# Moving GpSimd's arithmetic of a four-layer diffusion trunk to VectorE and ScalarE, RWKV's r, k and v as four-pass products, and its decay without own token as a shifted copy

## The chip, the core and the metric

The kernel runs on one core of one Trainium2 chip. The metric is the device time of one execution in microseconds; the time before is the median of three runs. Engines are named as the profile names them: PE is TensorE's matmul, PEld its weight load, DVE VectorE, ACT ScalarE, POOL GpSimd and SP the SyncE queue, which issues most DMAs.

## What is computed

One serving step of a trunk of four layers over 128 context and 128 latent tokens (two "sequences" s) of width 1024, all in float32. Layer 0 mixes tokens by a gated DeltaNet, layer 1 by neighbourhood attention, layer 2 by latent attention, layer 3 by RWKV-7; each layer ends in a SwiGLU feed-forward network. What bears on the change:

```
deltanet: q, k, v, z = split(h @ w_in); q, k, v = silu(dwconv3(q, k, v)); q, k = l2norm(q) * d**-0.5, l2norm(k)
          o = chunked gated delta rule, both directions (a triangular solve in it)
          out = (rmsnorm(o, out_norm) * silu(z)) @ w_out
rwkv:     xx = mean of both neighbours - h;  x_i = h + xx * mu_i   for i = r, k, v, w, a, g
          r, k, v = x_r @ W_r, x_k @ W_k, x_v @ W_v;  w, a, g by low-rank products (loras)
          decay = exp(-KAPPA * sigmoid(w)), cumulated over the tokens; vector-valued delta state, both directions
attention: p = softmax(s);  o = p @ v
```

## The kernel before

The program first records all its instructions on a tape, and a planner (class `Plan`) then sets the order of issue on each engine: a list schedule by rank (length of the rest of the chain) over costs that `Plan.costs` gives to each instruction, with pools of tiles (`ROOM`: 25 of 1024 columns, 28 of 512, seven PSUM banks) as a limit. So every instruction's engine and cost bear on the order of all of them. Each engine works through its instructions in order. All instructions are issued from one line (L2040), so the rows are told apart by shape, not by line.

**Products.** A large product runs as three passes of a faster matmul type (`F32R`): both sides are split into a rounded part `hi` (ScalarE copy) and a rest `lo` (VectorE, `raw - hi`), and hi·hi, hi·lo and lo·hi are summed in PSUM. `split` (L261) and `weight` (L270) do so for weights, `split_T` (L361) for activations. `linear` (L292) walks over chunks of 512 outputs and k; `linear_k` (L319) over k outermost with four accumulators (two sequences by two halves of 512). `linear_k` does RWKV's r, k and v projections (`project`, 8 k-tiles of 128x1024 each) and the second half of each feed-forward network. Products of plain float32 operands, as the loras', run as four passes, which the trace shows as two records.

```
nc.tensor.matmul(acc[s][c], xh, hi[:, 0, w], start=(k == 0), stop=False)
nc.tensor.matmul(acc[s][c], xh, lo[:, 0, w], start=False, stop=False)
...
nc.tensor.matmul(acc[s][c], xl, hi[:, 0, w], start=False, stop=(k == nk - 1))
```

**DeltaNet** (`deltanet_`, L626). After a chunk of q, k or v is projected, `evac` (L722) transposes it, copies it to SBUF (ScalarE), forms the convolution's middle and left tap on VectorE and the right one in two steps on GpSimd, takes SiLU, transposes back, and copies the result on VectorE. z is multiplied by the output norm's gain on GpSimd. `decays` (L761) adds a mask to four tiles of 128x1024, `unit` (L774) scales q, both on GpSimd. `inverses` (L572) inverts triangular blocks: a forward substitution of 31 steps, two VectorE instructions each (`substitute`, L524), between stream transposes, then small-tile products (`inverse_64`, L541) whose result VectorE negates.

**Attention** (`attend`, L915). Twelve calls in each of the two attention layers; each ends by copying the transposed probabilities from PSUM on VectorE.

**RWKV** (`rwkv_`). From the normed rows it forms `hx` and `xx`, and at once the split mix for k (`mk`). `mixed` forms x_i for one half g of the columns: on VectorE four instructions of 128x256, on GpSimd two of 128x1024; GpSimd has the loras' second half and all of r and v (`POOLMIX`). `mixes` splits them. Then: loras w and a; k projection; `rw_decays` (cumulative sum, and exponentials with and without the own token); `rw_keys`; r projection; lora g; `rw_products`; the inverse of the first half of the heads; v projection; queries; `rw_core` twice, with `fill` (the modulation's weights) between; the second half of the heads; the output products. `rw_keys` (half of it), `rw_queries` and the bonus in `rw_out` run on GpSimd.

Of the kernel before, what the change touches and what calls it, by code (L numbers as in the profile page):

```python
# [96 lines left out]
class Trunk:  # L97
# [163 lines left out]
    def split(self, raw, shape, pool=False):  # L261
# [4 lines left out]
        (nc.gpsimd if pool else nc.vector).tensor_tensor(lo, raw, hi.bitcast(F32), op=OP.subtract)  # L266
        self.free(raw)
        return hi, lo

    def weight(self, pieces, nk, width, pool=False):  # L270
# [7 lines left out]
        return self.split(raw, [128, nk, width], pool)  # L278
# [13 lines left out]
    def linear(self, W, chunks, xs, evac, lags=None, pool=()):  # L292
# [7 lines left out]
        for s, t in steps:  # L300
            ci, k0, n = units[t]
            width = sum(b - a for a, b in chunks[ci])
            if t not in held:
                held[t] = self.weight([W[k0 * 128:(k0 + n) * 128, a:b] for a, b in chunks[ci]], n, width, t in pool)
# [14 lines left out]
    def linear_k(self, W, xs, evac, lags=None, done=None, pool=()):  # L319
# [6 lines left out]
        for s, k in self.order(nk, 2, lags):  # L326
            if k not in held:
                held[k] = self.weight([W[k * 128:(k + 1) * 128, :]], 1, 1024, pool=k in pool)
            hi, lo = held[k]
            xh, xl = xs[s](k)  # L330
            for c in range(2):
                w = slice(c * 512, c * 512 + 512)
                nc.tensor.matmul(acc[s][c], xh, hi[:, 0, w], start=(k == 0), stop=False)
                nc.tensor.matmul(acc[s][c], xh, lo[:, 0, w], start=False, stop=False)
            for c in range(2):
                w = slice(c * 512, c * 512 + 512)
                nc.tensor.matmul(acc[s][c], xl, hi[:, 0, w], start=False, stop=(k == nk - 1))
# [15 lines left out]
    def to_T(self, src, n, hi, lo):  # L353
# [5 lines left out]
        self.split_T(p, n, hi, lo)  # L359

    def split_T(self, p, n, hi, lo):  # L361

        v = p[:, :n * 128].rearrange("p (a b) -> p a b", b=128)
        self.nc.scalar.activation(hi, v, AF.Copy)
        self.nc.vector.tensor_tensor(lo, v, hi.bitcast(F32), op=OP.subtract)
# [139 lines left out]
class DeltaNet:  # L505
# [35 lines left out]
    def inverse_64(self, Dc, DTc, AT, up, out):  # L541
# [13 lines left out]
        with self.scope():  # L555
# [10 lines left out]
            for B in range(2):  # L566
                a, b = (2 * B, 2 * B + 1) if not up else (2 * B + 1, 2 * B)
                c = 32 * (b % 2)
                nc.vector.tensor_scalar(out[32 * a:32 * a + 32, :, c:c + 32],
                                        py[32 * a:32 * a + 32, :].rearrange("p (m c) -> p m c", c=32), -1.0, None, op0=OP.mult)  # L570
# [55 lines left out]
    def deltanet_(self, l):  # L626
# [5 lines left out]
        r = self.g([72, 128])  # L632
        nc.gpsimd.dma_start(r, I["dn_conv"][j].rearrange("w (c p) -> (w c) p", p=128))
        p = self.ps()
        nc.tensor.transpose(p[:, :72], r, self.ident[:72, :72])
        cw = self.g([128, 3, 24])
        nc.vector.tensor_copy(cw.rearrange("p w c -> p (w c)"), p[:, :72])
# [6 lines left out]
        ona = self.g([128, 128])  # L644
        self.bcast_row(ona, I["dn_out_norm"][j])
# [7 lines left out]
        nc.gpsimd.tensor_tensor(wgl, wg, wgh.bitcast(F32), op=OP.subtract)  # L653
# [68 lines left out]
        def evac(ci, s, ps):  # L722
            which, half = ci // 2, ci % 2
            if which == 3:
                nc.scalar.activation(zs[s][half].rearrange("p a b -> p (a b)"), ps, AF.Silu)
                nc.gpsimd.tensor_tensor(zs[s][half], zs[s][half], ona[:, None, :].to_broadcast([128, 4, 128]), op=OP.mult)
                return
            with self.scope():
# [5 lines left out]
                x = self.g([128, 4, 128])  # L734
# [6 lines left out]
                y = self.g([128, 4, 127])  # L741
                nc.gpsimd.tensor_tensor(y, x[:, :, 1:], cw[:, 2, ci * 4:ci * 4 + 4, None].to_broadcast([128, 4, 127]), op=OP.mult)
# [1326 lines left out]
```

## Time and profile before

| | |
|---|---|
| median of 3 runs | 1763.6 us (1759.65 to 1768.04) |
| profiled execution | 1756.56 us, span 1754.6 us |
| mean granted TensorE clock | 0.952 |
| busy: PE, DVE, ACT, POOL | 1606.4, 1222.1, 826.5, 209.9 us |
| arithmetic on POOL | 89 TENSOR_TENSOR, 146.9 us |

The profile is of one execution. Busy is the time in which an engine had an instruction under way; a window is a stretch of the span, with the busy time of each engine in it. The clock is the share of 2.4 GHz that was granted to TensorE. A group of instructions has its busy time, the mean of one, and the idle time just before them with what ended it.

### The profile page before, as it was taken

The page shows a single profiled execution, that of the slowest core. Times are in us where ns is not written, and L with a number is a line of the kernel's source. Part 1 is how long each engine was busy: PE and PEld are TensorE (multiplying, and loading weights), DVE is VectorE, ACT ScalarE, POOL GpSimd, SP SyncE. Part 2 cuts the span into 40 slices and gives each one's busy share as a digit, 9 for nine tenths or more (in the row PEclk, how much of TensorE's full clock was granted, in tenths as well). Part 3 has the DMA queues.
Part 4 walks back from the last instruction along what each step waited for, and adds up shares of the span by engine and source line. Part 5 has one row for each costly group of instructions (what it writes and reads, how often), then busy time and mean ns, then how long its engine had stood idle before and what let it go on. Part 6 is the DMA issues. An engine that isn't in the chain of part 4 may idle for free. (4 is left out here: it accounts for less than half of the span.)

```text
span 1754.6 us, 25240 instructions
## 1 busy us (share of the span) xinstructions
PE 1606.4 (92%) x9492; PEld 1240.1 (71%) x9492; DVE 1222.1 (70%) x2369; ACT 826.5 (47%) x1400; POOL 209.9 (12%) x198
## 2 busy tenths in 40 slices
PE   6988799999999999999999999997729969989998
PEld 2765377887777778877777788875527858868886
DVE  3798888554596885446899744578986897585454
ACT  3666255443464564334665543444423722454343
POOL 2235110000002000000000000013630521000000
PEclk9989889999999999999999999998869879999999
DMA  9524959536567885366686744571511241336453
GB/s 360 186 90 139 363 189 325 195 129 210 208 256 242 304 295 181 131 216 232 243 340 211 253 156 161 203 264 49 193 59 50 83 150 49 121 103 204 156 181 132
DMA packets 130602, 333.86 MB, mean 190 GB/s; under 512 B 18305, under 2 KB 32450, under 8 KB 119216
## 3 DMA queue, kind: packets, MB, share of 16 engines
q1 hardware_dynamic: 123888, 311.33, 50.4%
q0 software_dynamic: 6592, 20.92, 3.9%
q8 instruction: 74, 1.21, 0.3%
q14 instruction: 48, 0.39, 0.1%
HBM read 328.31 MB, written 3.90 MB: 189 GB/s over the span
## 5 line engine op out<-in xcount | busy, mean ns | idle before, releaser
L2040 PE MATMUL v<-v,v 128*128 128x512 f32 (+11 forms) x9460 | 1598.7, 368 | 139.0 <-DVE v L2040 90.1
L2040 PEld LDWEIGHTS v<-v,v 128*128 128x128 f32 (+5 forms) x9460 | 1234.1, 172 | 502.2 <-DVE v L2040 120.7
L2040 DVE TENSOR_TENSOR v<-v,v 128x1024 fp32r<-128x1024 f32 (+19 forms) x1258 | 909.2, 748 | 452.2 <-ACT v L2040 267.5
L2040 ACT ACTIVATE v<-v 128x1024 fp32r<-128x1024 f32 (+13 forms) x991 | 694.2, 737 | 867.3 <-PE v L2040 392.9
L2040 POOL TENSOR_TENSOR v<-v,v 128x512 f32<-128x512 f32 (+3 forms) x89 | 146.9, 1671 | 227.3 <-ACT v L2040 127.4
L2040 POOL DMA_DIRECT2D v<-v x22 | 12.0, 548 | 666.9 <-PE v L2040 373.9
L2040 ACT ACTIVATE v<-v,v,v 128x128 f32<-128x128 f32 (+2 forms) x136 | 55.4, 474 | 28.1 <-DVE v L2040 27.3
L2040 ACT ACTIVATE v<-v,v 128x128 f32<-128x128 f32 (+1 forms) x144 | 52.7, 426 | 28.7 <-DVE v L2040 20.5
L2040 DVE TENSOR_SCALAR v<-v,v 128x128 f32<-128x128 f32 (+2 forms) x116 | 48.5, 456 | 10.1 <-ACT v L2040 9.6
L2040 DVE SCALAR_TENSOR_TENSOR v<-v,v,v 128x128 f32<-128x128 f32 (+3 forms) x120 | 51.4, 479 | 1.2 <-PE v L2040 0.9
L2040 DVE TENSOR_SCALAR v<-v 128x4 int32<-128x4 int32 (+10 forms) x206 | 43.7, 218 | 12.2 <-ACT v L2040 8.2
L2040 DVE TENSOR_REDUCE v<-v 128x4 f32<-128x512 f32 (+4 forms) x76 | 46.6, 626 | 5.1 <-ACT v L2040 2.6
L2040 POOL MEMSET v<- 128x512 f32 (+3 forms) x26 | 15.5, 614 | 250.4 <-PE v L2040 125.0
L2040 DVE COPY v<-v 128x512 f32<-128x512 f32 (+7 forms) x72 | 32.4, 468 | 18.3 <-PE v L2040 18.0
L2040 DVE SCALAR_TENSOR_TENSOR v<-v,v 128x8 f32<-128x8 f32 (+7 forms) x156 | 39.9, 265 | 1.9 <-ACT v L2040 0.2
L2040 ACT ACT_TABLE_LOAD x22 | 28.2, 1283 | 1.1 <-PEq L2059 0.7
L2040 DVE STREAM_TRANSPOSE v<-v 128x1024 f32<-128x1024 f32 x12 | 23.8, 2006 | 6.1 <-ACT v L2040 3.0
L2040 DVE SCALAR_TENSOR_TENSOR v<-v 128x1 f32<-128x1 f32 (+4 forms) x171 | 26.2, 159 | 2.4
L2040 DVE TENSOR_SCALAR v<-v,v,v 128x128 f32<-128x128 f32 x64 | 24.4, 404 | 2.7 <-PE v L2040 2.1
L2040 DVE TENSOR_TENSOR v<-v 128x1 f32<-128x1 f32 (+4 forms) x74 | 12.5, 170 | 10.1 <-ACT v L2040 9.1
L2040 POOL DMA_DIRECT2D v<-cache_na_k x1 | 1.2, 1185 | 144.8 <-DMA v<-ada_w 144.8
L2040 POOL DMA_DIRECT2D v<-rw_w x5 | 3.4, 676 | 99.6 <-DVE v L2040 99.6
(40 smaller groups left out, 93.1 us busy)
## 6 DMA issues: line engine op xcount, KB each, us to landing
v<-ada_w SPq DMA_DIRECT2D x88, 1024.0 KB
v<-ffn_w_in SPq DMA_DIRECT2D x160, 512.0 KB
v<-ffn_w_out SPq DMA_DIRECT2D x88, 512.0 KB
v<-dn_w_in SPq DMA_DIRECT2D x32, 512.0 KB
v<-na_w_qkv SPq DMA_DIRECT2D x24, 512.0 KB
v<-rw_w_rkv SPq DMA_DIRECT2D x24, 512.0 KB
v<-v POOLq DMA_DIRECT2D x20, 512.0 KB, 7.2
v<-ada_w SPq DMA_DIRECT2D x16, 512.0 KB
```

What stands on the lines that cost most here:

```text
L2040: ins = getattr(getattr(nc, engine), method)(*[real(a) for a in args], **{k: real(a) for k, a in kw.items()}).ins
```

## The change

GpSimd loses all its arithmetic (it keeps memsets and DMA issues), to VectorE or ScalarE; some work goes from VectorE to ScalarE; the projections of r, k and v take weights and mixes unsplit, in four passes; the decay without the own token is taken from the decay with it, shifted by a token, with the first column from one small exponential; the planner's costs for stream transposes and scans rise. The diff, cut to its core:

```diff
-    def weight(self, pieces, nk, width, pool=False):
+    def raw_weight(self, pieces, nk, width):
         raw = self.g([128, nk, width])
...
+        return raw
+    def weight(self, pieces, nk, width):
+        return self.split(self.raw_weight(pieces, nk, width), [128, nk, width])
...
@@ linear_k
+                held[k] = (self.raw_weight if whole else self.weight)([W[k * 128:(k + 1) * 128, :]], 1, 1024)
+            halves = [slice(c * 512, c * 512 + 512) for c in range(2)]
+            if whole:
+                for c, w in enumerate(halves):
+                    nc.tensor.matmul(acc[s][c], xs[s](k), held[k][:, 0, w], start=(k == 0), stop=(k == nk - 1))
...
@@ split_T
+            self.nc.scalar.activation(hi, v, AF.Copy, scale=gain)
+            self.nc.vector.scalar_tensor_tensor(lo, v, gain, hi.bitcast(F32), op0=OP.mult, op1=OP.subtract)
...
@@ inverse_64
-                nc.vector.tensor_scalar(out[32 * a:32 * a + 32, :, c:c + 32],
-                                        py[...], -1.0, None, op0=OP.mult)
+                nc.scalar.activation(out[32 * a:32 * a + 32, :, c:c + 32], py[...], AF.Copy, scale=-1.0)
@@ deltanet_
+        nc.gpsimd.dma_start(r[72:73], I["dn_out_norm"][j:j + 1])
-        self.bcast_row(ona, I["dn_out_norm"][j])
-        nc.gpsimd.tensor_tensor(wgl, wg, wgh.bitcast(F32), op=OP.subtract)
+        nc.vector.tensor_tensor(wgl, wg, wgh.bitcast(F32), op=OP.subtract)
...
-                nc.gpsimd.tensor_tensor(zs[s][half], zs[s][half], ona[:, None, :].to_broadcast([128, 4, 128]), op=OP.mult)
...
-                nc.scalar.activation(x, p.rearrange("p (a b) -> p a b", b=128), AF.Copy)
+                x = p.rearrange("p (a b) -> p a b", b=128)
-                    nc.vector.tensor_scalar(cv[:, i], x[:, i], cw[:, 1, c:c + 1], None, op0=OP.mult)
+                    nc.scalar.activation(cv[:, i], x[:, i], AF.Copy, scale=cw[:, 1, c:c + 1])
-                nc.gpsimd.tensor_tensor(y, x[:, :, 1:], cw[:, 2, ci * 4:ci * 4 + 4, None].to_broadcast([128, 4, 127]), op=OP.mult)
-                nc.gpsimd.tensor_tensor(cv[:, :, :127], cv[:, :, :127], y, op=OP.add)
+                    nc.vector.scalar_tensor_tensor(cv[:, i, :127], x[:, i, 1:], cw[:, 2, c:c + 1], cv[:, i, :127], op0=OP.mult, op1=OP.add)
-                nc.vector.tensor_copy(dst, p)
+                nc.scalar.activation(dst, p, AF.Copy)
...
-                    nc.gpsimd.tensor_tensor(e, e, self.K(f"madd{d}")[:, None, :].to_broadcast([128, 8, 128]), op=OP.add)
+                    nc.vector.tensor_tensor(e, e, self.K(f"madd{d}")[:, None, :].to_broadcast([128, 8, 128]), op=OP.add)
...
+                    for h in range(8):
+                        nc.scalar.activation(t[:, h], t[:, h], AF.Copy, scale=rn[:, w, h:h + 1])
...
-                self.to_T(ob[...], 4, oT[0][g][:, :, s, :], oT[1][g][:, :, s, :])
+                self.to_T(ob[...], 4, oT[0][g][:, :, s, :], oT[1][g][:, :, s, :], onc)
@@ attend
-            nc.vector.tensor_copy(pt.rearrange("p b q -> p (b q)"), t)
+            nc.scalar.activation(pt.rearrange("p b q -> p (b q)"), t, AF.Copy)
@@ rwkv_
-        mk = [[self.g([128, 4, 2, 128], F32R) for _ in range(2)] for _ in range(2)]
+        mk = [self.g([128, 4, 2, 128]) for _ in range(2)]
...
-                    nc.scalar.activation(hi, xm, AF.Copy)
-                    nc.vector.tensor_tensor(lo, xm, hi.bitcast(F32), op=OP.subtract)
...
-            if eng is nc.gpsimd:
-                eng.tensor_tensor(flat(xm), flat(xx[g]), m, op=OP.mult)
-                eng.tensor_tensor(flat(xm), flat(xm), flat(hx[g]), op=OP.add)
...
+                nc.vector.scalar_tensor_tensor(xm[:, kk], xx[g][:, kk], mu[:, i, k:k + 1], hx[g][:, kk], op0=OP.mult, op1=OP.add)
...
         def mixes(i):
-                m.append(self.split(xm, [128, 4, 2, 128]))
+            return [mixed(i, g) for g in range(2)]
...
+            self.linear_k(I["rw_w_rkv"][j, i], xs, evac, lags, done, whole=True)
@@ rw_decays
-        nc.vector.tensor_tensor(seq(sg), seq(cm), seq(sg), op=OP.subtract)
-            nc.scalar.activation(AR[s][:, :, 0], sg[:, :, s], AF.Exp, scale=-KAPPA / 2)
+        nc.scalar.activation(first, mid.rearrange("p (c s) -> p c s", s=2), AF.Exp, scale=KAPPA / 2)
@@ rw_keys
-            nc.vector.tensor_tensor(AR[s][:, :, 0], kkT[s], AR[s][:, :, 0], op=OP.mult)
+            nc.vector.tensor_tensor(AR[s][:, :, 0, to], kkT[s][:, :, to], AR[s][:, :, 1, fro], op=OP.mult)
+            nc.vector.tensor_tensor(AR[s][:, :, 0, edge], kkT[s][:, :, edge], first[:, :, s], op=OP.mult)
-        nc.gpsimd.tensor_tensor(fl(kd), fl(kd), fl(cm), op=OP.mult)
+        nc.vector.tensor_tensor(fl(kd), fl(kd), fl(cm), op=OP.mult)
...
@@ rw_queries (all five products and sums), rw_out (two): nc.gpsimd becomes nc.vector
@@ Plan.costs
-                t = 68 + n * (0.52 if one else 1.042)
+                t = 68 + n * {"transpose": 1.75, "tensor_tensor_scan": 2.07}.get(method, 0.52 if one else 1.042)
```

## Rows read from the trace of the kernel before

**Rows 1.** Page of the profile, part 1: busy us, share of the span, instructions.
```profile
PE 1606.4 (92%) x9492; PEld 1240.1 (71%) x9492; DVE 1222.1 (70%) x2369; ACT 826.5 (47%) x1400; POOL 209.9 (12%) x198
```

**Rows 2.** Windows: stretch, length, busy us of PE, PEld, DVE, ACT, POOL (instructions), clock, DMA.
```profile
60.00:240.00 180.00, 151.14 (x1044) 108.34 (x1045) 157.19 (x345) 96.20 (x160) 64.02 (x51) 0.88 0.53 188
820.00:980.00 160.00, 152.96 (x946) 112.20 (x945) 146.81 (x575) 99.51 (x242) 5.49 (x11) 0.98 0.76 277
1180.00:1320.00 140.00, 84.72 (x413) 61.09 (x412) 128.08 (x163) 57.76 (x117) 61.02 (x34) 0.80 0.27 95
1340.00:1480.00 140.00, 123.02 (x1226) 102.55 (x1226) 113.27 (x202) 53.63 (x112) 44.17 (x43) 0.83 0.26 88
...
1180.00:1200.00 20.00, 10.20 (x43) 7.62 (x41) 19.96 (x17) 3.45 (x5) 17.88 (x8) 0.87 0.00 2
```

**Rows 3.** Waits: who for whom, us in total, times, longest.
```profile
PE v L2040 <- DVE v L2040: 93.7, 38, 31.6
```

**Rows 4.** Timeline of TensorE, 1150 to 1345 us: start, length, what, idle time before.
```profile
1318.10 4.00 PE L2040 MATMUL v<-v,v 128*128 128x512 f32 x10 [31.60 <-DVE v L2040]
```

**Rows 5.** Timeline of VectorE, 1170 to 1345 us; x counts the instructions merged.
```profile
1174.61 1.22 DVE L2040 TENSOR_TENSOR v<-v,v 128x1024 fp32r<-128x1024 f32 x1
...
1188.16 6.62 DVE L2040 SCALAR_TENSOR_TENSOR v<-v,v,v 128x256 f32<-128x256 f32 x3
...
1202.56 0.47 DVE L2040 SCALAR_TENSOR_TENSOR v<-v,v,v 128x256 f32<-128x256 f32 x1
...
1284.40 38.18 DVE L2040 TENSOR_TENSOR v<-v,v 128x31 f32<-128x31 f32 x67
...
1326.63 1.83 DVE L2040 TENSOR_TENSOR v<-v,v 128x1024 fp32r<-128x1024 f32 x2
```

**Rows 6.** Timeline of GpSimd, 1170 to 1345 us.
```profile
1183.24 16.05 POOL L2040 TENSOR_TENSOR v<-v,v 128x1024 f32<-128x1024 f32 x7 [0.55 <-PE v L2040]
...
1284.91 12.88 POOL L2040 TENSOR_TENSOR v<-v,v 128x512 f32<-128x512 f32 x10
```

**Rows 7.** Groups of instructions, VectorE, 1180 to 1300 us: busy us, mean ns, idle before.
```profile
L2040 DVE TENSOR_TENSOR v<-v,v 128x1024 fp32r<-128x1024 f32 x12 | 22.6, 1888 | 1.9 <-ACT v L2040 1.2 <-PE v L2040 0.6
L2040 DVE SCALAR_TENSOR_TENSOR v<-v,v,v 128x256 f32<-128x256 f32 x12 | 17.6, 1506 | 0.0
...
L2040 DVE SCALAR_TENSOR_TENSOR v<-v,v 128x1024 f32<-128x1024 f32 x2 | 5.7, 2844 | 0.0
```

**Rows 8.** Groups of instructions, GpSimd, 1180 to 1300 us.
```profile
L2040 POOL TENSOR_TENSOR v<-v,v 128x1024 f32<-128x1024 f32 x16 | 37.5, 2361 | 72.8 <-ACT v L2040 34.5 <-DMA v<-ada_w 27.4 <-DVE v L2040 10.2
L2040 POOL TENSOR_TENSOR v<-v,v 128x512 f32<-128x512 f32 x14 | 20.4, 1485 | 0.3
```

**Rows 9.** Groups of instructions, VectorE and ScalarE, whole span.
```profile
L2040 DVE TENSOR_TENSOR v<-v,v 128x512 f32<-128x512 f32 x298 | 198.4, 693 | 118.1 <-PE v L2040 106.7 <-DMA v<-na_rel_bias 6.0 <-ACT v L2040 3.2
...
L2040 DVE COPY v<-v 128x512 f32<-128x512 f32 x38 | 25.0, 680 | 2.9 <-PE v L2040 2.7
...
L2040 ACT ACTIVATE v<-v 128x512 f32<-128x512 f32 x238 | 139.3, 608 | 193.2 <-PE v L2040 141.7 <-DVE v L2040 39.0 <-POOL v L2040 8.8
...
L2040 ACT ACTIVATE v<-v,v 128x128 f32<-128x128 f32 x80 | 25.4, 382 | 13.3 <-DVE v L2040 9.8 <-POOL v L2040 3.6
```

**Rows 10.** Groups of instructions, TensorE, 660 to 680 us and 1270 to 1290 us.
```profile
L2040 PE MATMUL v<-v,v 128*128 128x512 f32 x88 | 20.6, 394 | 0.0
...
L2040 PE MATMUL v<-v,v 128*128 128x256 f32 x16 | 3.6, 379 | 0.0
```

**Rows 11.** Groups of instructions, VectorE, 60 to 200 us.
```profile
L2040 DVE TENSOR_TENSOR v<-v,v 128x1024 fp32r<-128x1024 f32 x21 | 33.4, 1605 | 4.8 <-ACT v L2040 4.5
L2040 DVE TENSOR_SCALAR v<-v,v 128x128 f32<-128x128 f32 x58 | 26.4, 508 | 9.7 <-ACT v L2040 9.6
L2040 DVE SCALAR_TENSOR_TENSOR v<-v,v,v 128x127 f32<-128x127 f32 x48 | 13.8, 340 | 0.1
```

**Rows 12.** Groups of instructions, GpSimd, 60 to 240 us.
```profile
L2040 POOL TENSOR_TENSOR v<-v,v 128x508 f32<-128x508 f32 x24 | 32.1, 1353 | 80.9 <-ACT v L2040 61.9 <-DVE v L2040 19.0
```

More of the change, by code (lines that the diff above doesn't have):

```diff
@@ L258, in gate, with split @@
         return t
-    def split(self, raw, shape, pool=False):
+    def split(self, raw, shape):
         nc = self.nc
@@ L303, in linear @@
             if t not in held:
-                held[t] = self.weight([W[k0 * 128:(k0 + n) * 128, a:b] for a, b in chunks[ci]], n, width, t in pool)
+                held[t] = self.weight([W[k0 * 128:(k0 + n) * 128, a:b] for a, b in chunks[ci]], n, width)
             hi, lo = held[t]
@@ L317, in linear, with linear_k @@
                 evac(ci, s, acc[s])
-    def linear_k(self, W, xs, evac, lags=None, done=None, pool=()):
+    def linear_k(self, W, xs, evac, lags=None, done=None, whole=False):
         nc = self.nc
@@ L327, in linear_k @@
             if k not in held:
[L328 to L337, printed above, removed]
+                held[k] = (self.raw_weight if whole else self.weight)([W[k * 128:(k + 1) * 128, :]], 1, 1024)
[3 more added lines that the diff above has]
+                    nc.tensor.matmul(acc[s][c], xs[s](k), held[k][:, 0, w], start=(k == 0), stop=(k == nk - 1))
+            else:
+                hi, lo = held[k]
+                xh, xl = xs[s](k)
+                for c, w in enumerate(halves):
+                    nc.tensor.matmul(acc[s][c], xh, hi[:, 0, w], start=(k == 0), stop=False)
+                    nc.tensor.matmul(acc[s][c], xh, lo[:, 0, w], start=False, stop=False)
+                for c, w in enumerate(halves):
+                    nc.tensor.matmul(acc[s][c], xl, hi[:, 0, w], start=False, stop=(k == nk - 1))
             if s == 1:
@@ L351, in h_of, with to_T @@
         return [lambda k, s=s: (ht[0][k // 4][:, k % 4, s, :], ht[1][k // 4][:, k % 4, s, :]) for s in range(2)]
-    def to_T(self, src, n, hi, lo):
+    def to_T(self, src, n, hi, lo, gain=None):
         nc = self.nc
@@ L568, in inverse_64 @@
                 c = 32 * (b % 2)
-                nc.vector.tensor_scalar(out[32 * a:32 * a + 32, :, c:c + 32],
-                                        py[32 * a:32 * a + 32, :].rearrange("p (m c) -> p m c", c=32), -1.0, None, op0=OP.mult)
+                nc.scalar.activation(out[32 * a:32 * a + 32, :, c:c + 32],
+                                     py[32 * a:32 * a + 32, :].rearrange("p (m c) -> p m c", c=32), AF.Copy, scale=-1.0)
     def inverses(self, ATs):
@@ L1283, in mixes, with project @@
         def mixes(i):
[L1284 to L1290 removed]
+            return [mixed(i, g) for g in range(2)]
+        def project(i, m, lags=None):
             tok = [[self.g([128, 512]) for _ in range(2)] for _ in range(2)] if i < 2 else [self.g([128, D]) for _ in range(2)]
[L1292 removed]
+            xs = [lambda k, s=s: m[k // 4][:, k % 4, s] for s in range(2)]
             def evac(c, s, ps):
@@ L1299, in done @@
                     self.free(m[k // 4])
-            self.linear_k(I["rw_w_rkv"][j, i], xs, evac, lags, done, pool)
+            self.linear_k(I["rw_w_rkv"][j, i], xs, evac, lags, done, whole=True)
             return tok
@@ L1320, in keys @@
         def keys(g, F):
-            for f in F:
-                self.rw_keys(g, f, kT[g], kkT[g])
+            for d in range(2):
+                self.rw_keys(g, d, F[d], kT[g], kkT[g])
             self.free(kT[g], kkT[g])
```

97 lines of the change are left out of this document (41 added, 56 removed).

## The prediction

> **What bounds the kernel now.** I began with the page's busy times: TensorE is busy for 92% of the span and VectorE for 70% [rows 1], so the kernel is bound by TensorE nearly everywhere, and what can be won are the some 148 us of the span in which TensorE has nothing to do. The windows say where those lie [rows 2]: 29 us in DeltaNet (60 to 240 us), 7 in the end of neighbourhood attention and the latent one (820 to 980), 55 in the front of RWKV (1180 to 1320) and 17 in its second half (1340 to 1480). In the front of RWKV VectorE is busy for 128 of 140 us and the granted clock averages 0.80: there VectorE is the bound. The waits agree: TensorE stood 93.7 us for VectorE, 31.6 us of them in one piece [rows 3], and the timeline puts that piece at 1286 to 1318 us, in the middle of the forward substitution of the first RWKV inverse [rows 4, 5].
>
> Why is VectorE so slow there? In 1180 to 1200 us it runs 17 instructions in 20 us, with GpSimd busy for 17.9 us [rows 2]. The timeline gives the same forms with and without company: three mixes of 128x256 take 6.62 us while GpSimd works [rows 5, 6], one of the same form takes 0.47 us after GpSimd has stopped, and a split of 128x1024 takes 1.22 us. So GpSimd's tensor_tensors hold VectorE up, and the price can be read by form [rows 7]: 12 splits at 1.89 instead of 1.22 us (8.0 us), 12 mixes at 1.51 instead of 0.47 (12.4 us), two 128x1024 products at 2.84 instead of 1.22 (3.2 us). The substitution (67 instructions, 38.2 us) has 12.9 us of GpSimd beside its first part [rows 5, 6]; I take 9 us of it as stretch. Some 7 us are in smaller forms, as far as I read them. Together about 40 us of VectorE's 128.
>
> **The change, part by part.**
>
> **A. Front of RWKV, 1180 to 1327 us.** Out of VectorE: the 40 us of stretch; the 12 splits of weights and mixes in the stretch at 1.22 us (14.6 us), two subtractions of the decays at 1.22 (2.4 us) and a key-mix split at 0.7. Into VectorE from GpSimd [rows 8]: of its 16 operations of 128x1024, 14 are seven mixes done in two steps, which become 7 x 4 at 0.47 (13.2 us); two remain as products at 1.22 (2.4 us); 14 of 128x512 at 0.69 (9.7 us, [rows 9]). 128 - 40 - 18 + 25 = 95 us instead of 128. ScalarE loses a copy for each split, eight exponentials in all and gains a few of 128x8; it was busy for 58 of 140 us [rows 2] and stays off the path.
>
> TensorE pays: 24 k-tiles x 2 sequences x 2 halves = 96 products change from three passes into four. The split passes run at 20.6 us / 88 = 0.234 us each, 0.70 a product [rows 10]. The four-pass price is in the trace only at 256 columns, as two records of 3.6 / 16 = 0.225 us for a product [rows 10], so 4 x 0.225 = 0.90 us at 512 columns; the lower end is the clock alone, 4 x 512 columns at 2.4 GHz = 0.853 us. That is 15 to 19 us in all; I take 18, since the row has its overhead in it. Nearly all of it falls into stretches where TensorE now idles. The second effect is larger: a product of r, k or v no longer waits for a split by ScalarE and VectorE, only for its weight's landing and its mix. During the substitution VectorE can do no splits, which is why TensorE stands for 31.6 us although part of the value projection is still undone (splits follow at 1326 us and later [rows 5]); afterwards these products can run under the substitution.
>
> So the stretch has floors of about 95 us (VectorE) and 84.7 + 18 = 103 us (TensorE) less what a fuller TensorE gets back in clock: 0.20 of 84.7 is 17 us at most [rows 2]. 140 - 100 = **40 us gained**. Ends: 55 us (all idle time of the stretch, and the clock pays for the extra passes), 15 us (the chain norm, loras, decays, key projection, keys, products, substitution keeps its length but for what of the stretch lies on it).
>
> What GpSimd does is the point at which a page speaks against the change. The Trainium skill (Perfetto Trace Analysis, section Optimizing Scalar/DVE Operations) says that where VectorE is saturated, giving work to ScalarE or even GpSimd can pay, and warns in the same place that the two share a port, so that it may not help. By the first half of that sentence taking GpSimd's work back would cost the 25 us and win nothing; that is the third rival below. The skill (SBUF — State Buffer, section Who interferes with whom) calls the port an exclusive lock in which the second one to come waits for the whole instruction. By that the stretch would be up to GpSimd's own busy time there, 37.5 + 20.4 = 58 us, instead of 40; the trace shows less, and the sum would be the same, because TensorE's floor of 100 us decides then.
>
> **B. DeltaNet, 60 to 240 us.** VectorE is busy for 157 of 180 us [rows 2]. Out: stretch of the 21 splits, 21 x (1.605 - 1.22) = 8.1 us; 48 of the 58 scalings of the convolution, 48 x 0.508 = 24.4 us; 12 copies at 0.68, 8.2 us; 4 negations in the inverse at some 0.68, 2.7 us. In: 48 more convolution taps at 0.340 (16.3 us), four decay masks and a gate split at 1.22 (6.1 us) [rows 9, 11]. Net 157 - 43 + 22 = 136 us. GpSimd's two steps of 1.35 us in each of the 12 convolution calls [rows 12] also go out of a chain that ends in a transpose. ScalarE takes 48 scalings at 0.38, 16 head scalings at 0.38, 12 copies at 0.61 and a few more, and loses 12 copies: 96 + 28 = 124 of 180 us. That is allowed, but its queue is in order, and the convolution now reads its input from PSUM for as long as four scalings and eight taps last, so a bank is given back later. TensorE idles 29 us here, also for other reasons. I take **12 us** of it; ends 25 and 0. The output gain as a scale of the split after the transpose, instead of a product on GpSimd, and the norm's row in the convolution's transpose instead of a broadcast, are under this work and cost nothing; their cover is the projection, and bare they would be 2 us.
>
> **C. Attention.** 24 copies of probabilities go from VectorE (0.68) to ScalarE (0.61) [rows 9]. In 820 to 980 us VectorE is busy for 147 of 160 and ScalarE for 100, TensorE idles 7: **3 us**, ends 5 and 0.
>
> **D. Rest of RWKV, 1340 to 1480 us.** The stretch by GpSimd (44 us busy) goes, but queries, keys and the output's bonus, all GpSimd's, come to VectorE, 30 x 0.69 = 21 us less 7 for a subtraction and the negations. The second substitution loses cover: value products that fed TensorE after 1327 us are already done. One against the other I take **0**, ends a gain of 12 and a loss of 15. The shifted decay itself replaces an exponential and a subtraction by two column writes; it shortens the chain by about 2 us, within A.
>
> GpSimd's queue keeps only memsets and DMA issues, which so come earlier; SP's keeps its order, and a raw weight holds one buffer where three were needed, so the loads can run ahead. The planner's costs change too (transposes and scans dearer), so the order of issue is another everywhere, which no row prices: it is why the range is wide.
>
> **Sum.** 40 + 12 + 3 + 0 = 55 us. The profiled execution took 1756.6 us (span 1754.6 and 2.0 around it), the median of the runs is 1763.6, 7 us above. 1756.6 - 55 = 1701.6, plus 7: **1709 us**, 3.1% less. A measurement here can tell about 0.5%, 9 us.
>
> **Rivals.**
> 1. TensorE takes over earlier. The order puts the longer products where TensorE is already full, and the chain before the substitution keeps 20 us of its idle time: 84.7 + 18 + 20 = 123 of 140, 17 us gained, 7 in B, 3 in C. 1763.6 - 27 = 1737 us. For it: TensorE is at 92%. Against: the idle time sits just where the products are.
> 2. Slower. All products of r and v run before the substitution, now that nothing holds them; then the 31.6 us of idle time stay, and the 18 us of extra passes lie in front, up to twice that where the clock is granted at half. Of the stretch only 9 us in the substitution and 5 elsewhere on the path come back: + 26 - 14 = + 12, 1776 us. It decides from the point at which fewer than about 15 of the 64 r and v products (14 us) are left when the substitution starts. Against: the key projection and its chain come first in rank, and 64 x 0.90 = 58 us of products don't fit ahead of it.
> 3. The offload was worth it: VectorE's long instructions are not GpSimd's doing. Then A is 128 - 18 + 25 = 135 of 140, 5 us, B 3 and C 2 us: 1754 us. Against it stand the durations with and without GpSimd [rows 5, 6].
>
> **Chances.** Forecast 0.68, rival 1 0.17, rival 2 0.09, rival 3 0.06. Faster by over 0.5%: 0.68 + 0.17 = 0.85; within: 0.06; slower: 0.09. The range goes from all good ends together (55 + 25 + 5 + 12 = 97 us, 1667, rounded to 1668) to rival 3, 1754; rival 2 and a small rest are left out.
>
> **What would show it.** Right: GpSimd without tensor_tensors, mixes of 128x256 at 0.47 us and splits at 1.22 throughout; no wait of over 15 us of TensorE for VectorE in RWKV's first half; four-pass records of 512 columns at some 0.45 us, two a product; the stretch from RWKV's norm to the first small-tile products about 40 us shorter. Wrong: a hole as long as the substitution on TensorE (rival 2), VectorE as full as before (rival 3), or TensorE full while the layer's length hardly shrinks (rival 1).

## The result, and the profile of the changed kernel

The changed kernel took 1685.4 us (median of 4 runs, 1679.4 to 1688.5), the kernel before 1761.6 us beside it (4 runs, 1755.4 to 1768.0): a ratio of 0.956, 95% interval 0.952 to 0.961, 76 us less. Forecast were 55 us less, 1709; the change brought 21 us more. The profiled execution is the slowest of the four, 1688.5 us with a span of 1686.7, so what follows explains the 67.9 us between the two spans.

The page's busy times of the changed kernel:

```profile
PE 1587.1 (94%) x9396; PEld 1206.5 (72%) x9396; DVE 1128.2 (67%) x2364; ACT 830.3 (49%) x1466; POOL 63.3 (4%) x109
```

Against [rows 1] GpSimd's busy time went from 210 to 63 us, all of it memsets and DMA issues, and VectorE's fell by 94 us though it took over most of the arithmetic. TensorE's idle time is 1686.7 - 1587.1 = 99.6 us instead of 148.2, and its busy time is 19.3 us less, although four-pass products add to it. So 49 of the 67.9 us are idle time that went, and 19 are TensorE needing less time for its work, at a granted clock of 0.969 over the span instead of 0.952.

Where they lie is seen in windows cut at the layers: DeltaNet, RWKV from its norm to the end of the two transposes behind the first substitution, where the small-tile products of the inverse begin (its front), and the rest of RWKV. The columns are the stretch, its length, busy time and instructions of each engine, granted clock, share and rate of the DMAs. First the kernel before:

```profile
7.80:284.50 276.70, 239.24 (x1547) 165.66 (x1547) 215.87 (x484) 143.03 (x236) 73.58 (x68) 0.91 0.65 230
1157.70:1326.50 168.80, 111.74 (x571) 79.76 (x569) 154.97 (x224) 73.60 (x153) 61.02 (x34) 0.83 0.36 130
1326.50:1553.50 227.00, 207.53 (x2209) 174.43 (x2209) 174.21 (x317) 92.52 (x169) 44.69 (x44) 0.89 0.30 96
```

and the same stretches of the changed one:

```profile
7.90:266.80 258.90, 228.16 (x1610) 156.94 (x1610) 191.01 (x473) 161.18 (x303) 17.79 (x33) 0.96 0.77 278
1148.40:1262.80 114.40, 114.39 (x542) 65.06 (x541) 96.86 (x229) 48.29 (x127) 5.68 (x7) 1.00 0.37 134
1262.80:1484.90 222.10, 195.15 (x2120) 160.12 (x2118) 174.82 (x345) 89.94 (x170) 9.14 (x17) 0.89 0.34 115
```

RWKV's front is 54 us shorter, the rest of RWKV 5, DeltaNet 18, together 77. The stretch from neighbourhood to latent attention, with the feed-forward network between them, is 7.4 us longer. Before:

```profile
485.60:963.00 477.40, 465.96 (x2563) 355.57 (x2561) 352.51 (x933) 254.53 (x496) 17.07 (x28) 1.00 0.68 239
```

After:

```profile
468.10:952.90 484.80, 461.23 (x2480) 354.40 (x2476) 337.06 (x900) 261.33 (x512) 17.04 (x28) 0.97 0.64 220
```

For this stretch one trace doesn't settle the sign. Two runs described below (`dummy_write`, `dummy_read`) keep the changed kernel's order of issue on every engine and differ from it only by work on GpSimd that comes later. In their traces the same stretch, cut at the same instructions, takes 473.2 and 477.6 us:

```profile
470.20:943.40 473.20, 454.67 (x2472) 351.88 (x2476) 336.58 (x901) 260.36 (x512) 17.00 (x28) 0.99 0.64 225
471.40:949.00 477.60, 457.37 (x2472) 353.92 (x2476) 336.58 (x901) 260.50 (x512) 17.00 (x28) 0.98 0.64 223
```

The three other feed-forward networks are each longer by under 1 us.

In the front TensorE is now busy for all of 114.4 us at a granted clock of 1.00, where it was busy for 111.7 of 168.8 at 0.83. Its timeline (start, duration, first instruction, count, the idle time before it) is one piece until the inverse is under way:

```profile
1139.71 125.86 PE L2032 MATMUL v<-v,v 128*128 128x512 f32 x705
1266.20 53.31 PE L2032 MATMUL v<-v,v 32*32 32x32 f32 x480 [0.64 <-ACT v L2032]
...
1352.18 4.83 PE L2032 MATMUL v<-v,v 32*32 32x32 f32 x160 [21.89 <-DVE v L2032]
```

The hole of 31.6 us [rows 4] under the first substitution is gone. One of 21.9 us stands before 1352 us, under the second substitution. In the list of waits it is half of what is left for VectorE (93.7 us, longest 31.6, in [rows 3]):

```profile
PE v L2032 <- DVE v L2032: 44.5, 24, 21.9
```

VectorE's groups in the front show what it was freed from (columns as in [rows 7]); before,

```profile
L2040 DVE TENSOR_TENSOR v<-v,v 128x1024 fp32r<-128x1024 f32 x22 | 34.8, 1584 | 2.8 <-ACT v L2040 2.1 <-PE v L2040 0.6
...
L2040 DVE SCALAR_TENSOR_TENSOR v<-v,v,v 128x256 f32<-128x256 f32 x12 | 17.6, 1506 | 0.0
...
L2040 DVE TENSOR_TENSOR v<-v,v 128x512 fp32r<-128x512 f32 x4 | 4.9, 1236 | 0.0
```

and after, where no split is left in this stretch and 40 instructions of the mixes' form take less than 12 did:

```profile
L2032 DVE SCALAR_TENSOR_TENSOR v<-v,v,v 128x256 f32<-128x256 f32 x40 | 16.5, 478 | 0.1
```

Its timeline shows a wait of 9.5 us for ScalarE's share of the key projection, where the longest wait in the front before was 3.2 us, and a substitution of 23.4 us for 62 instructions, against 38.2 for 67 [rows 5]:

```profile
1188.02 0.69 DVE L2032 TENSOR_TENSOR v<-v,v 128x512 f32<-128x512 f32 x1 [9.54 <-ACT v L2032]
...
1235.48 23.35 DVE L2032 TENSOR_TENSOR v<-v,v 128x31 f32<-128x31 f32 x62
```

### The profile page after: what moved, and what is told of

It reads as the page before. It is cut to its first block, busy times and chain, and to the rows that moved or that the text cites. A ratio compares the mean times of both kernels' runs of the same rounds, so it can differ in the third digit from the quotient of the medians.

```text
span 1686.7 us, 24968 instructions
## 1 busy us (share of the span) xinstructions
PE 1587.1 (94%) x9396; PEld 1206.5 (72%) x9396; DVE 1128.2 (67%) x2364; ACT 830.3 (49%) x1466; POOL 63.3 (4%) x109
## 3 DMA queue, kind: packets, MB, share of 16 engines
q8 instruction: 74, 1.21, 0.3%
## 4 chain that ended last, share of the span: by engine, by line
PE 73%; DVE 12%; DMA 8%; ACT 5%; issue 2%; SPq 0%; ACTq 0%; DVEq 0%
PE v L2032 73%; DVE v L2032 12%; DMA v<-ada_w 5%; ACT v L2032 4%; DMA v<-ffn_w_out 2%; DMA v<-na_w_qkv 1%; DMA v<-dn_w_in 1%; ACT L2032 0%; DMA v<-ffn_w_in 0%; SPq L2032 0%; ACTq L2057 0%; ACTq L2032 0%; DVEq L2032 0%
## 5 line engine op out<-in xcount | busy, mean ns | idle before, releaser
L2032 PE MATMUL v<-v,v 128*128 128x512 f32 (+13 forms) x9364 | 1582.6, 369 | 94.1 <-DVE v L2032 44.5
L2032 PEld LDWEIGHTS v<-v,v 128*128 128x128 f32 (+6 forms) x9364 | 1200.4, 170 | 473.2 <-issue 148.7
L2032 DVE TENSOR_TENSOR v<-v,v 128x512 f32<-128x512 f32 (+19 forms) x1271 | 864.4, 705 | 477.5 <-ACT v L2032 280.8
L2032 ACT ACTIVATE v<-v 128x512 f32<-128x512 f32 (+9 forms) x989 | 679.1, 721 | 797.2 <-PE v L2032 373.6
L2032 ACT ACTIVATE v<-v,v 128x128 f32<-128x128 f32 (+2 forms) x212 | 77.3, 413 | 30.4 <-PE v L2032 12.5
L2032 DVE SCALAR_TENSOR_TENSOR v<-v,v,v 128x127 f32<-128x127 f32 (+4 forms) x200 | 66.9, 381 | 7.1 <-ACT v L2032 6.1
L2032 DVE TENSOR_SCALAR v<-v 128x1 int32<-128x1 int32 (+9 forms) x194 | 32.8, 175 | 9.1 <-ACT v L2032 6.1
L2032 DVE SCALAR_TENSOR_TENSOR v<-v,v 128x1 f32<-128x1 f32 (+7 forms) x156 | 32.6, 218 | 4.8 <-ACT v L2032 2.2
L2032 DVE STREAM_TRANSPOSE v<-v 128x1024 f32<-128x1024 f32 x12 | 23.4, 2003 | 3.8 <-ACT v L2032 3.6
L2032 DVE TENSOR_SCALAR v<-v,v 128x512 f32<-128x512 f32 (+2 forms) x68 | 24.6, 395 | 0.4
L2032 DVE COPY v<-v 128x32 f32<-128x32 f32 (+9 forms) x34 | 7.5, 223 | 12.8 <-PE v L2032 12.6
L2032 ACT ACTIVATION_READ_ACCUMULATOR v<-v,v 128x1 f32 x64 | 13.3, 208 | 0.0
```

The lines of the kernel that those rows point to most:

```text
L2032: ins = getattr(getattr(nc, engine), method)(*[real(a) for a in args], **{k: real(a) for k, a in kw.items()}).ins
```

## Experiments

All times are medians beside runs of the kernel before on the same chip; "after" is the changed kernel with its 76 us. The kernel's planner writes the order of issue anew for every edit unless the text says otherwise.

**The two halves of the change.** The first run keeps everything but the unsplit products; the second is the kernel before with nothing but them.

```diff
 three_pass (edit of the changed kernel, cut; the key mix is split in the same way)
-            return [mixed(i, g) for g in range(2)]
+            return [self.split(mixed(i, g), [128, 4, 2, 128]) for g in range(2)]
...
-            self.linear_k(I["rw_w_rkv"][j, i], xs, evac, lags, done, whole=True)
+            self.linear_k(I["rw_w_rkv"][j, i], xs, evac, lags, done)
 four_pass (edit of the kernel before, cut; GpSimd keeps its work)
-                m.append(self.split(xm, [128, 4, 2, 128]))
...
+            return [mixed(i, g, nc.gpsimd if i in POOLMIX else nc.vector) for g in range(2)]
...
-            self.linear_k(I["rw_w_rkv"][j, i], xs, evac, lags, done, pool)
+            self.linear_k(I["rw_w_rkv"][j, i], xs, evac, lags, done, whole=True)
```

> The changed kernel, but with r, k and v as three-pass products of split weights and mixes (the splits on ScalarE and VectorE), so that the move off GpSimd, the shifted decay and the new costs stand alone. My theory, that GpSimd's company on VectorE was the main cost, expects 1700 to 1715 us: some 50 of the 76 us stay, and TensorE waits again for splits while a substitution runs (a hole of 10 to 25 us in the first one). The rival, that the unsplit products were the main gain because they need neither VectorE nor ScalarE, expects 1730 to 1745 us.

> The kernel before, with nothing changed but r, k and v as four-pass products of unsplit weights and mixes (GpSimd keeps all its work). My theory expects 1735 to 1750 us: the splits leave VectorE and the hole under the first substitution fills, but mixes and small instructions stay stretched. The rival (unsplit products are the main gain) expects 1700 to 1715 us. A third reading, that four passes only cost, expects 1765 to 1780 us.

Without the four-pass products: 1705.1 us against 1763.5, ratio 0.968 (0.964 to 0.972), 58 us less. With them alone: 1743.6, ratio 0.988 (0.985 to 0.992), 20 us less. Both are what was expected if GpSimd's company was the main cost. The two add to 78 us where the whole change brought 76: the parts add up within the measurement. The products are worth having alone though they are longer. The rest, about three quarters of the gain, is GpSimd's work together with what went from VectorE to ScalarE; no run takes these two apart for the whole kernel. That GpSimd's company had stretched the splits is seen in the first run, where VectorE does them still. From RWKV's norm to 1300 us they take 1.22 us each, against 1.58 in the front before:

```profile
L2037 DVE TENSOR_TENSOR v<-v,v 128x1024 fp32r<-128x1024 f32 x27 | 32.3, 1219 | 4.1 <-ACT v L2037 2.2 <-issue 1.6
```

TensorE's timeline of the first run shows what the splits hold up, a hole under the first substitution:

```profile
1258.00 78.58 PE L2037 MATMUL v<-v,v 128*128 128x512 f32 x844 [22.22 <-DVE v L2037]
```

In the second run GpSimd's arithmetic still stands beside the substitution. VectorE's timeline has it at 36.9 us for the 62 instructions that took 23.4 above:

```profile
1258.74 36.91 DVE L2038 TENSOR_TENSOR v<-v,v 128x31 f32<-128x31 f32 x62
```

That is 13.6 us of stretch in one piece, where I had taken 9.

**What GpSimd does to VectorE.** To the changed kernel, with its order of issue kept, idle work on GpSimd was added beside RWKV's key path behind one small sum, once reading SBUF and once only writing it; the results are not used.

```diff
+            calls += [lambda: nc.gpsimd.tensor_tensor(spare[:, :], real(a), real(b), op=OP.add)] * 45     # dummy_read
+            calls += [lambda: nc.gpsimd.memset(spare[:, :], 0.0)] * 90                                   # dummy_write
```

> The changed kernel in the same order of issue, with 45 idle-work sums of 128x256 put into GpSimd's queue right behind the rsqrt of the key norms in RWKV's front; they read two tiles in SBUF and write a spare one, and nothing waits for them but the reuse of what they read. If GpSimd's reads from SBUF hold VectorE up, the two-input VectorE instructions beside them (products of 128x512 at 0.69 us, of 128x1024 at 1.22, mixes at 0.47) take up to twice as long or more, VectorE's chain to the first substitution grows by 8 to 25 us and the kernel with it by 5 to 20 us. If the long instructions of the kernel before were late inputs or misread records, their lengths stay and the time is the same within 3 us.

> As the run with idle sums, but 90 memsets of 128x256 that only write, after one small sum. If it is the reading that collides, VectorE's instructions with two inputs keep their lengths (0.69, 1.22, 0.47 us) and the time is the same within 4 us. If any company of GpSimd slows VectorE, lengths and time grow as with the sums.

With the reads 1711.5 us, 26 above after (ratio to before 0.972, 0.966 to 0.977); with the writes 1684.0, as after (0.954, 0.950 to 0.959). GpSimd's timeline of the first and VectorE's beside it:

```profile
1190.05 50.27 POOL L2042 TENSOR_TENSOR spare<-v,v 128x256 f32<-128x256 f32 x45
```

```profile
1195.00 6.56 DVE L2034 TENSOR_TENSOR_SCAN v<-v,v 128x512 f32<-128x512 f32 x4
...
1204.95 6.29 DVE L2034 SCALAR_TENSOR_TENSOR v<-v,v 128x512 f32<-128x512 f32 x5
...
1226.61 6.13 DVE L2034 SCALAR_TENSOR_TENSOR v<-v,v,v 128x256 f32<-128x256 f32 x7
```

The same instructions beside the memsets:

```profile
1184.41 34.00 POOL L2042 MEMSET spare<- 128x256 f32 x90
```

```profile
1188.93 4.55 DVE L2034 TENSOR_TENSOR_SCAN v<-v,v 128x512 f32<-128x512 f32 x4
...
1196.02 3.63 DVE L2034 SCALAR_TENSOR_TENSOR v<-v,v 128x512 f32<-128x512 f32 x5
...
1210.96 2.85 DVE L2034 SCALAR_TENSOR_TENSOR v<-v,v,v 128x256 f32<-128x256 f32 x7
```

Scans, products of 512 columns and mixes are longer by 44 to 115% beside the reads and unchanged beside the writes (4.56, 3.62 and 2.85 us in after). The edits differ in nothing but this idle work, so it is shown that GpSimd's reading of SBUF slows these instructions of VectorE here.

The 26 us of the whole kernel are not its price alone, though. Beside the reads ScalarE stands until GpSimd's last sum is done, and VectorE's transposes ahead of the substitution then wait for ScalarE:

```profile
1240.36 9.40 ACT L2034 ACTIVATE v<-v 32x128 f32<-32x128 f32 x37 [27.71 <-POOL spare L2042]
```

```profile
1247.21 3.85 DVE L2034 STREAM_TRANSPOSE v<-v 128x1024 f32<-128x1024 f32 x2 [5.40 <-ACT v L2034]
```

Beside the memsets the same copies wait 9.2 us for VectorE, and the transposes 0.6 for ScalarE. The likely reason is that the tiles which the sums read can't be used again before the sums are done; the expectation had named this. From the end of the key norms to its last instruction before the transposes VectorE takes 52.6 us beside the reads and 36.6 beside the memsets, 16 us more (expected were 8 to 25), and that is stretch; some 5 us of the later start of the substitution are the wait. The Trainium skill (SBUF — State Buffer, section Who interferes with whom) says that a VectorE instruction with two inputs in SBUF contends with a GpSimd instruction that reads SBUF and not with one that only writes it; by that rule, the two runs agree on both sides for these three forms. Other forms differ: a 128x1024 instruction with two inputs took 1.21 us beside the reads and 1.22 beside the memsets, and two one-input instructions of 128x1024 took 2.15 us together beside the reads, 1.70 beside the memsets and 1.42 in after.

**DeltaNet by itself.** The changed kernel with DeltaNet's mixer as it was before, GpSimd's part included (the negations in the inverse stay on ScalarE).

```diff
-    def deltanet_(self, l):       # the changed one
+    def deltanet_(self, l):       # the one before, whole
```

> The changed kernel with the whole DeltaNet mixer as before (its convolution tap, masks, gains and scaling on GpSimd). The DeltaNet layer went from 277 to 259 us; if that was this part, 12 to 20 us come back: 1698 to 1706 us, with scalings and splits stretched again between 60 and 200 us. If the order of issue made it, the layer stays at about 259 us.

1710.5 us, ratio 0.970 (0.966 to 0.974), 25 above after; the sign as expected, the size more. The 21 splits between 60 and 220 us take 1.57 us each again, 1.22 in after. DeltaNet's own stretch is 22 us longer, with TensorE at a clock of 0.88 instead of 0.96 and busy 7 us more:

```profile
7.80:289.00 281.20, 235.25 (x1544) 165.29 (x1545) 210.98 (x476) 140.28 (x234) 70.81 (x58) 0.88 0.62 222
```

**One projection split.** The value projection alone, then the key projection alone, back in three passes.

```diff
-            self.linear_k(I["rw_w_rkv"][j, i], xs, evac, lags, done, whole=True)
+            self.linear_k(I["rw_w_rkv"][j, i], xs, evac, lags, done, whole=i != 2)     # v_split, with its mixes split
+            self.linear_k(I["rw_w_rkv"][j, i], xs, evac, lags, done, whole=i != 1)     # k_split, with its mixes split
```

> The changed kernel with the value projection alone back to three passes of split operands. If the products run under the first substitution because they wait for no split, the hole returns there: 5 to 15 us slower, 1690 to 1700 us, with a wait of TensorE for VectorE of more than 10 us. If only the length of TensorE's work counts there, the 32 products are 5 us shorter and the kernel 0 to 5 us faster.

> The changed kernel with the key projection alone back to three passes. In the changed kernel TensorE is busy without a gap from RWKV's norm to the first inverse and VectorE idles for 9.5 us under the key projection; if TensorE is the bound there, this is 3 to 6 us faster (32 products at 0.16 us). If the start of the projection then waits for the splits of mix and weights, it is the same or up to 8 us slower.

1701.9 us (0.965, 0.962 to 0.968), 16 above after, and 1698.8 us (0.963, 0.960 to 0.966), 13 above. The first time is just above what was expected, but not for the reason given. Under the first substitution TensorE has six gaps of 10 us together, the longest 3.3 us, mostly for modulation weights; the long hole is under the second, 29 us where after has 22:

```profile
1235.07 1.72 PE L2032 MATMUL v<-v,v 128*32 128x512 f32 x8 [3.30 <-DMA v<-ada_w]
...
1354.71 5.09 PE L2032 MATMUL v<-v,v 128*32 128x512 f32 x28 [29.05 <-DVE v L2032]
```

The second was expected to be up to 6 us faster or 8 slower and is a miss. Stages that the edit doesn't touch differ too: with the value split latent attention is 10.5 us shorter than in the trace of after. Only part of that can be the planner's new order, since in the traces of `dummy_write` and `dummy_read`, with after's own order, it is 6 to 7 us shorter as well. So how much of the 16 and 13 us is the splits' own stays open.

**The hole under the second substitution.** SP's queue in the changed kernel explains why no modulation weights are there to fill it. Its waits between 1310 and 1400 us (us, times, longest), and its issues:

```profile
SPq L2032 <- DVE v L2032: 34.5, 5, 27.8
```

```profile
1326.95 3.72 SPq L2032 DMA_DIRECT2D v<-ada_w  x3
1330.77 0.39 SPq L2032 DMA_DIRECT2D v<-rw_w_out  x1
1359.09 1.04 SPq L2032 DMA_DIRECT2D v<-v  x2
```

The store of a modulation group's rows is queued on SP and waits for VectorE, which is in the substitution; the weights of the next group stand behind it for 27.8 us. Two runs take that away: one moves the store to GpSimd's queue, one also lets ScalarE read the group's sum out of PSUM so that it needn't wait for VectorE.

```diff
-                nc.sync.dma_start(self.gd[l, g - 1, m]...
+                nc.gpsimd.dma_start(self.gd[l, g - 1, m]...             # store_only and fill_hole
-        nc.vector.tensor_tensor(s, p, b, op=OP.add)
+        nc.scalar.activation(s, p, AF.Copy)                             # fill_hole
+        nc.vector.tensor_tensor(s, s, b, op=OP.add)                     # fill_hole
```

> The changed kernel, with the modulation groups' sums taken from PSUM by ScalarE (VectorE adds the bias afterwards) and their two row stores issued on GpSimd's queue instead of SP's. In the changed kernel SP's queue stands 27.8 us for VectorE behind such a store while the second substitution runs, no weights of the last modulation group arrive and TensorE idles 21.9 us. If that is why nothing fills the hole, its products (64 records, some 9 us) move into it and the kernel is 5 to 12 us faster. If the hole has no work that could fill it, the time is the same within 4 us.

> The changed kernel with only the row stores of the modulation groups moved from SP's queue to GpSimd's; the sums stay on VectorE. SP then doesn't stand for VectorE, so the last group's weights arrive during the second substitution, but its products still wait for the one PSUM bank that VectorE empties. In the run that filled the hole the small-tile products afterwards ran at half clock; if that was because the last group's products no longer lay among them, here they still do: same as the changed kernel within 4 us or up to 6 us faster, and the 50 us after the hole at a granted clock of 0.84 or more. If the order of issue alone made that run slow, nothing of the clock follows and the time can lie 10 us to either side.

Filled, the hole brought nothing: 1692.3 us over six executions (1681.6 to 1707.7), 1685.9 without the longest, at a ratio of 0.959 (0.954 to 0.965). The six lie in two groups: three took 1681.6 to 1685.9 us at a mean granted clock of 0.965 to 0.969, three 1698.6 to 1707.7 at 0.952 to 0.958. The traced one, 1698.6, is of the longer group. The longest wait of TensorE for VectorE is 4.2 us in it, but the gain is given back right behind it. The windows of this execution,

```profile
1320.00:1340.00 20.00, 13.35 (x72) 3.44 (x71) 18.35 (x50) 1.58 (x3) 0.54 (x1) 0.67 0.91 337
...
1360.00:1380.00 20.00, 20.00 (x116) 18.32 (x117) 5.85 (x10) 1.18 (x2) 1.61 (x3) 0.50 0.17 46
1380.00:1400.00 20.00, 20.00 (x101) 16.34 (x99) 10.85 (x26) 4.92 (x7) 1.33 (x3) 0.50 0.17 54
```

of after,

```profile
1320.00:1340.00 20.00, 8.40 (x76) 6.04 (x76) 17.41 (x38) 6.28 (x14) 0.54 (x1) 0.76 0.77 298
...
1360.00:1380.00 20.00, 20.00 (x186) 16.63 (x186) 14.34 (x25) 5.55 (x9) 3.73 (x7) 0.84 0.66 207
1380.00:1400.00 20.00, 20.00 (x187) 15.55 (x184) 13.94 (x30) 4.50 (x6) 2.69 (x5) 0.96 0.74 264
```

and of the run with the store alone:

```profile
1320.00:1340.00 20.00, 0.07 (x4) 0.00 (x0) 18.28 (x51) 0.00 (x0) 0.00 (x0) 0.55 0.26 100
...
1360.00:1380.00 20.00, 20.00 (x158) 15.09 (x156) 12.44 (x29) 2.88 (x4) 3.19 (x6) 0.83 0.82 290
1380.00:1400.00 20.00, 20.00 (x171) 15.20 (x171) 14.37 (x33) 4.55 (x7) 3.26 (x6) 1.00 0.50 173
```

In the traced execution of the filled run TensorE is busy for all of 1360 to 1400 us and has a granted clock of 0.50, which is 1.2 GHz: the modulation products went into the hole, and the inverse's and the cores' products follow without them. One form of those in the filled run,

```profile
L2033 PE MATMUL v<-v,v 128*128 128x64 f32 x54 | 12.1, 420 | 0.0
```

and the same form and the modulation products (second line) in after:

```profile
L2032 PE MATMUL v<-v,v 128*128 128x64 f32 x96 | 12.5, 284 | 0.0
L2032 PE MATMUL v<-v,v 128*32 128x512 f32 x64 | 7.5, 597 | 0.0
```

54 products take 12.1 us where 96 took 12.5. In after the 64 modulation products lie among them, and the clock is 0.84 and 0.96. With the store alone SP no longer stands for VectorE, the hole remains (22.9 us), the modulation products lie at 1359 to 1387 us again, the clock is 0.83 and 1.00, and the time is that of after: 1686.4 us (0.956, 0.953 to 0.959). So filling the hole's 22 us brought no gain. In the traced execution it came with 1.2 GHz right behind it; why the clock was not granted there stays open, since the order differs between the runs in more than this. The low clock is not the whole reason: the three shorter executions, at nearly the mean clock of after (0.969), are no faster than after's 1679.4 to 1688.5 us. No trace of them was kept, so where they give the 22 us back is not shown.

**Small parts.** The copies of probabilities back on VectorE, the decay without own token computed as before, and the planner's costs as before.

```diff
-            nc.scalar.activation(pt.rearrange("p b q -> p (b q)"), t, AF.Copy)
+            nc.vector.tensor_copy(pt.rearrange("p b q -> p (b q)"), t)                                   # attn_vector
-            nc.vector.tensor_tensor(AR[s][:, :, 0, to], kkT[s][:, :, to], AR[s][:, :, 1, fro], op=OP.mult)
...
+            nc.scalar.activation(AR[s][:, :, 0], sg[:, :, s], AF.Exp, scale=-KAPPA / 2)                   # old_decay
-                t = 68 + n * {"transpose": 1.75, "tensor_tensor_scan": 2.07}.get(method, 0.52 if one else 1.042)
+                t = 68 + n * (0.52 if one else 1.042)                                                    # old_costs
```

> The changed kernel with the 24 copies of attention probabilities back on VectorE. I had forecast 3 us of gain from their move; the two attention layers and the feed-forward between them became 7 us longer together (477 to 485 us). If the copies on ScalarE did that, this is 3 to 10 us faster than the changed kernel; if the order of issue and late weights did it, within 4 us either way.

> The changed kernel with the decay without own token by a subtraction and an exponential of its own, as before. TensorE is busy without a gap in RWKV's front, and VectorE and ScalarE are not; so the same within 4 us, or up to 5 us slower where the keys lie on the chain to the second substitution.

> The changed kernel planned with the costs of before for stream transposes and scans (2.0 and 1.2 us on the chip, planned as 1.1 and 0.6). Twelve and eight instructions; if they only shift some instructions, the same within 6 us; if the right costs helped the planner to cover the substitutions, 6 to 15 us slower.

1696.6 us (0.962, 0.960 to 0.965), 1685.4 (0.957, 0.954 to 0.961) and 1684.0 (0.954, 0.952 to 0.957). The shifted decay and the new costs are worth nothing that can be measured. The copies' run is a miss: against the trace of after the stretch of the attention layers got 6 us shorter with VectorE copying (478.6 us), but RWKV, whose code is the same, got 12 longer. The 6 us are no gain of VectorE's, for the two traces with after's own order were at 473.2 and 477.6 us there. Untouched stages differ by some 10 us between traces, where the planner orders anew (RWKV here) and also between executions of one order (the attention stretch), and differences of that size between two traces carry no cause.

## Why the prediction held, point by point

**Direction and mechanism.** The trace before had shown mixes at 1.51 us beside GpSimd's work and 0.47 without it, and the forecast rested on that. The signs named in advance are there: GpSimd without tensor_tensors, mixes at 0.48 us, splits at 1.22 (357 of them over the span), no hole over 15 us in RWKV's first half. Rival 3 (the offload was worth it) falls by the first half, 58 us less with GpSimd's work taken back and splits at 1.22 us, and by the two runs with idle work; rival 2 (slower) by the gapless timeline. Of rival 1 a part is true: TensorE is the bound of the front now, only at 114 us and not with 20 us of idle time. The range's lower end, 1763.6 - 97, is 1667 and not 1668, which changes nothing here.

**A, forecast 40 us, measured 54**, nearly the good end of 55. The term that was mis-sized is TensorE's floor: "0.20 of 84.7 is 17 us at most" was put down as what a fuller TensorE gets back in clock, and the floor of 100 us took 3 us of it. The clock went to 1.00 for the whole front. The groups of TensorE's products of 512 columns show it, before and after:

```profile
L2040 PE MATMUL v<-v,v 128*128 128x512 f32 x234 | 68.9, 449 | 52.7 <-DVE v L2040 52.2 <-ACT v L2040 0.4
...
L2040 PE MATMUL v<-v,v 128*32 128x512 f32 x88 | 11.7, 599 | 0.0
```

```profile
L2032 PE MATMUL v<-v,v 128*128 128x512 f32 x193 | 82.0, 577 | 0.0
...
L2032 PE MATMUL v<-v,v 128*32 128x512 f32 x24 | 2.8, 596 | 0.0
```

234 passes at the 0.234 us of [rows 10] would be 54.8 us and took 68.9: 14 us of clock in this group alone. After, 193 records are the 96 products of two records each and one more, so the r, k and v products are all done when the substitution ends, where the trace before records 234 of their 288 passes at most. Their price is read from the weight loads that open each record:

```profile
1161.44 0.19 PEld L2032 LDWEIGHTS v<-v,v 128*128 128x128 f32 x1 [0.24 <-issue]
1161.87 0.19 PEld L2032 LDWEIGHTS v<-v,v 128*128 128x128 f32 x1 [0.24 <-DVE v L2032]
```

They are 0.43 us apart, so 0.86 us a product, near the lower of my ends (0.853) and not the 0.90 that I took; the four passes cost (0.86 - 0.70) x 96 = 15 us, not 18. The forecast had not seen two moves: 64 modulation products (8.9 us) left the front, and the some 54 passes that the kernel before did behind it (12.6 us at 0.234) came in. Together that makes 111.7 + 15 + 12.6 - 8.9 = 130 us of TensorE's work at the old clock; 114.4 were measured. By this estimate some 16 us are clock, of at most 19 (0.17 of 111.7), and they pay for the extra passes, as the good end of A had it. That the two moves nearly cancel is luck.

VectorE's floor was off too: I counted the 12 splits after 1180 us; in the whole front there were 26, 39.7 us with their stretch, and it is busy for 97 us where 155 - 33 = 122 follow from the forecast. It idles now, so this made no time.

**The stretch in the substitution** was 14 us and not 9, by the second run.

**B, forecast 12 us, measured 18** between the profiles and 25 by the run with the old mixer. VectorE's saving in this stretch is 25 us (forecast 21 in a part of it). Mis-sized is again the clock: the sum took 12 of TensorE's idle time only, but of the 17.8 us 11 are busy time (239.2 to 228.2, granted clock 0.91 to 0.96) and 7 idle time.

**C, forecast 3 us gained: not decided.** The trace of after has a loss of 7 us there, the two with the same order a gain of 4 and none (473.2 and 477.6 against 477.4). TensorE's idle time from neighbourhood to latent attention rose in all three, from 11 us to 24, 19 and 20; its waits for ScalarE went from 3.9 to about 10 us, for VectorE from 1.3 to between 6.4 and 6.7. I had priced the copies alone. They are not shown to be the cause: with the copies on VectorE again the two waits are 7.9 and 13.1 us. What the order of issue does there stays open.

**D, forecast 0, measured a gain of 5.** TensorE's busy time fell by 12 us there (207.5 to 195.2). Some 9 of them are in the form of the value products (173 records of 128x512, 48.2 us, became 120, 39.6 us), which are now done in front. Its idle time rose by 7 (19.5 to 27), with the hole under the second substitution, the loss of cover that D had named.

**The shifted decay**, 2 us of chain forecast, is worth nothing measurable: the chain it shortens no longer sets the front's end, TensorE does.

## What to carry to other kernels

Compare an instruction's duration with and without another engine's company by form before counting what an offload saves; in RWKV's front GpSimd's arithmetic cost VectorE some 37 us of stretch (8.0 + 12.4 + 3.2 in three forms, 13.6 in the substitution) and, at the forecast's prices, took 25 us off it. A product that needs more passes but no preparation can win where the preparing engine is the bound, since it can run while that engine is busy. And when a stretch is to be filled, put the granted clock into the sum: 19 of the 68 us were TensorE's own busy time, although its four-pass products added 15. Before a stage's difference between two traces is given a cause, look at how far the stage differs between two executions of one program: here up to 12 of 480 us.

## What the runs showed of the hardware that was not expected

- Three of VectorE's two-input forms take 1.4 to 2.2 times their length beside GpSimd instructions that read SBUF, and 1.0 times beside memsets (scans 6.56 against 4.55 us, mixes 6.13 against 2.85). One of 128x1024 kept its 1.21 us.
- A TensorE that is busy for 40 of 40 us stood at a granted clock of 0.50 for all of them (traced execution of the filled run, 1360 to 1400 us).
- One small store that waits for a busy engine kept SP's queue, and the weight loads behind it, standing for 27.8 us; moving it to another queue alone changed the time by nothing.
